# Column sums of a conditioning vector: a rearrangement through DRAM and two four-column products in place of eight one-column products

## The chip, the cores and the metric

The kernel runs on one core of a Trainium2 chip. The metric is the device time of one execution in microseconds (us); the time before is the median of three runs. Five engines of the core work side by side, each through its own list of instructions in order: TensorE (PE, matrix products, with its weight loads listed as PEld), VectorE (DVE), ScalarE (ACT), GpSimd (POOL) and SyncE (SP, which here only issues DMA transfers). An instruction waits at the head of its list until the semaphores it asks for have been raised, and everything behind it on that engine waits with it.

## What is computed

The reference is one decoder block on a sequence of 256 tokens with 2048 channels. A conditioning vector `c` gives six modulation vectors of 2048 numbers each; they scale and shift the two normalisations and gate the two residual branches:

```python
c_act = jax.nn.silu(c)
mod = (c_act @ w_ada[l] + b_ada[l])[:, None, :]
sh1, sc1, g1, sh2, sc2, g2 = jnp.split(mod, 6, axis=-1)
h = rms_norm(x, norm1_g[l]) * (1.0 + sc1) + sh1
x = x + g1 * hybrid_mixer(h, ...)      # sparse attention and a state-space scan, merged, then w_out
h = rms_norm(x, norm2_g[l]) * (1.0 + sc2) + sh2
x = x + g2 * swiglu(h, w_gate[l], w_up[l], w_down[l])
```

All data are float32. The change touches only how `g1`, `sh2`, `sc2` and `g2` are summed. They are wanted late: `g1` first where the output projection `w_out` is added to x, `sc2` and `sh2` at the second normalisation, `g2` in the last projection.

## The kernel before

Nearly all the time goes into products of a weight matrix with the 256 tokens. Weights come in pieces of 128 x 2048 (1 MB, one `entry` each), loaded by SP into one of three `raw` buffers. ACT copies a piece rounded into `wh` (L181), DVE subtracts to get the remainder `wl` (L182); each has three buffers. PE then multiplies `wh` with a 512-column operand (both halves of the split tokens, L207) and `wl` with 256 columns (L208), 16 such pairs for a piece; where the operand is split otherwise, three products of 256 columns take their place (L210 to L212). `run_jobs` processes the entries two jobs ahead of the product. The sums land in four PSUM banks (`acc`); DVE and ACT evacuate them (L251, L252 and others). Smaller products use the four other banks (`ps_side`).

The later modulation is computed beside this, entry by entry. `bg` is a queue of 64 background entries, 8 for each of 8 groups: four vectors `v` in the order 0 (g1), 2 (sc2), 1 (sh2), 3 (g2), in two halves of 1024 channels. An entry is one 1 MB piece of `w_ada`, in the same `raw` buffers as the weights. `ada2_entry.fn` multiplies its two 128 x 1024 halves with columns of `cact` on DVE and adds them up in `acc2`, a tile with a single buffer (pool `bgp`), L430 and L432. After the eighth entry `acc2` holds, in each of 128 partitions, a partial sum for each of 1024 channels. What is left is a sum over partitions, and PE does it (L436): eight products, each with 128 channels of `acc2` as stationary operand and one column of ones as moving operand, into eight columns of a side bank, in which a partition then stands for a channel. A float32 product runs on PE as two passes with a weight load each, so a group has 16. DVE adds the bias into `mods` (L439) and in some groups scales (L442, L444). Where the entries are placed is set by the order of the program, but the order on each engine is made by a scheduler at build time, which pulls instructions ahead of others where it expects waits.

Names used later: a group is written as vector_half, so 1_1 is the second half of vector 1. `pb` is the state-space branch's projection; its accumulator is evacuated by L1052 (multiplied with a gate `sgr` that is loaded from DRAM), added to `pbacc` by L1053, and split into `mg` by ACT L255 and DVE L256. `out` is the `w_out` projection that follows and reads `mg`. `pa` is the attention branch's projection, evacuated by ACT L251 (`ev`) and DVE L252 (`sa`), then gated by L837. `gu` is the gate and up projection of the FFN.

Of the kernel before, what the change touches and what calls it, by code (L numbers as in the profile page):

```python
# [9 lines left out]
F32 = mybir.dt.float32  # L10
F32R = mybir.dt.float32r
AF = mybir.ActivationFunctionType
ALU = mybir.AluOpType
# [3 lines left out]
P = 128  # L17
# [30 lines left out]
def hybrid_block_kernel(  # L48
# [22 lines left out]
    nc = tc.nc  # L71

    act, dve, pool, pe = nc.scalar, nc.vector, nc.gpsimd, nc.tensor

    def open_pool(stack, name, bufs=1, space=None, side=None):
        kw = {} if space is None else {"space": space}
        if side:
            kw["side"] = side
        if name in ("pa1", "pa2", "pb1", "pb2", "pc", "pf", "psa", "pss", "pa"):
            kw["reuse_waits"] = "tile"  # L80
        return stack.enter_context(tc.tile_pool(name=name, bufs=bufs, **kw))

    cst = open_pool(ctx, "cst")
# [21 lines left out]
    dr = open_pool(ctx, "dr", 1, DRAM)  # L105
    bgp = open_pool(ctx, "bgp")
# [3 lines left out]
    def ps_side(name):  # L110
        return banks["side"].tile([P, 512], F32, tag="ps", name=name)
# [152 lines left out]
    ident = cst.tile([P, P], F32, name="ident")  # L264
    make_identity(nc, ident)
    ones = cst.tile([P, P], F32, name="ones")
    pool.memset(ones, 1.0)
    tri = mxp.tile([P, P], F32, name="tri")
    pool.affine_select(tri, ones, [[1, P]], ALU.is_ge, 0.0, base=0, channel_multiplier=-1)
    rb = cst.tile([32, 16], F32, name="rb")  # L270
    eps = cst.tile([P, 1], F32, name="eps")
    pool.memset(eps, EPS)
    cact = cst.tile([P, 16], F32, name="cact")
# [11 lines left out]
    dve.scalar_tensor_tensor(cact, ctmp, 1.0, cact, op0=ALU.add, op1=ALU.mult)  # L285
    dve.tensor_scalar(cc[:, C_CW : C_CB + 48], cc[:, C_CW : C_CB + 48], 0.5, None, op0=ALU.mult)

    d_z = dr.tile([32, P, L], F32, name="d_z")
    d_sa = dr.tile([16, P, L], F32, name="d_sa")
    d_x1 = dr.tile([16, P, L], F32, name="d_x1")  # L290
# [130 lines left out]
    def ada2_entry(v, half, g):  # L421
        def fn(raw):
            if g == 0:
                state["acc2"] = bgp.tile([P, 1024], F32, tag="acc2", name=f"acc2_{v}_{half}")
            a = state["acc2"]
            for j in range(2):
                k = 2 * g + j
                r = raw[:, 1024 * j : 1024 * j + 1024]
                if k == 0:
                    dve.tensor_scalar(a, r, cact[:, 0:1], None, op0=ALU.mult)  # L430
                else:
                    dve.scalar_tensor_tensor(a, r, cact[:, k : k + 1], a, op0=ALU.mult, op1=ALU.add)  # L432
            if g == 7:
                ps = ps_side(f"ada2_{v}_{half}")
                for b in range(8):
                    pe.matmul(ps[:, b : b + 1], a[:, b * P : b * P + P], ones[:, 0:1], start=True, stop=True)  # L436
                o = C_BADA + 16 * (v + 2) + 8 * half
                s = slice(8 * half, 8 * half + 8)
                dve.tensor_tensor(mods[:, v, s], ps[:, 0:8], cc[:, o : o + 8], op=ALU.add)  # L439
                if v == 2:  # L440
                    o = C_N2 + 8 * half
                    dve.scalar_tensor_tensor(a2[:, s], mods[:, 2, s], 1.0, cc[:, o : o + 8], op0=ALU.add, op1=ALU.mult)  # L442
                if v in (0, 3):
                    dve.tensor_scalar(mods[:, v, s], mods[:, v, s], 0.5, None, op0=ALU.mult)  # L444

        entries.append((ada2[16 * v + 8 * half + g], fn))
# [827 lines left out]
    for i, (a, b) in enumerate(OUTC):  # L1274
        eng, f = (pool, r) if a >= OUTP else (dve, rp)
        v = Fd["x2"][:, a:b]
# [112 lines left out]
```

## Time and profile before

| | us |
|---|---|
| median of 3 runs | 2046.61 (2041.5 to 2046.69) |
| the profiled execution | 2048.57 |
| its span, first to last instruction | 2046.9 |
| PE busy | 2011.2 (98%) |
| DVE busy | 1458.3 (71%) |
| ACT busy | 1048.8 (51%) |

The profiled execution took 2048.57 us, of which 1.67 us lie outside the span. A row of a timeline gives the start of a group of instructions of one line, its length, the engine, the line, what is written and read, the count, and in brackets the idle time of the engine ahead of it with what ended it. Lengths of PE rows overlap (an instruction starts before the one ahead of it has drained), so the time that PE needs for some instructions is the distance of the starts, not the sum of the lengths.

### The profile page before, as it was taken

What the parts mean: (1) busy time and instruction counts of PE and PEld (TensorE: products, weight loads), DVE (VectorE), ACT (ScalarE), POOL (GpSimd) and SP (SyncE); (2) the same over time, 40 slices, a digit from 0 to 9 for tenths busy, and PEclk for the clock granted to TensorE, in tenths of its full rate; (3) what the DMA queues carried; (4) which work ended last, traced back from release to release, by engine and by line L of the source; (5) the groups of instructions that cost most, each with busy time, mean ns of one, the idle gap of its engine ahead of it and who ended that gap; (6) DMA issues with size and microseconds to landing.
All of it is one profiled execution on the core that took longest, in us unless ns stands there. A gap on an engine that the chain in (4) does not pass through costs nothing.

```text
span 2046.9 us, 31891 instructions
## 1 busy us (share of the span) xinstructions
PE 2011.2 (98%) x12964; PEld 1794.5 (88%) x12964; DVE 1458.3 (71%) x1832; ACT 1048.8 (51%) x1427; POOL 187.0 (9%) x161
## 2 busy tenths in 40 slices
PE   8999999999999999999999999999999999999997
PEld 6899998899888888889989988888888888888887
DVE  6777787977678888988788765767776555544443
ACT  3665475565346776666664444544444444443442
POOL 0000000230000111100114224000000000000000
PEclk8999999999999999999999999999999999999999
DMA  9888767666887767766577876457775555565552
GB/s 365 331 302 306 269 230 270 218 227 242 300 316 268 255 245 259 255 227 240 210 260 250 283 239 212 166 208 290 259 286 206 185 185 185 200 214 186 187 187 97
DMA packets 102338, 492.29 MB, mean 241 GB/s; under 512 B 10768, under 2 KB 45952, under 8 KB 48688
## 3 DMA queue, kind: packets, MB, share of 16 engines
q1 hardware_dynamic: 100528, 486.19, 66.2%
q0 software_dynamic: 704, 3.15, 0.4%
q8 instruction: 102, 1.67, 0.3%
q10 hardware_dynamic: 960, 0.92, 0.1%
q14 instruction: 44, 0.36, 0.0%
HBM read 475.44 MB, written 17.92 MB: 241 GB/s over the span
## 4 chain that ended last, share of the span: by engine, by line
PE 91%; DVE 4%; DMA 2%; ACT 1%; issue 1%; POOL 0%; SPq 0%; DVEq 0%; POOLq 0%; ACTq 0%
PE acc_gu L207 15%; PE acc_cv L207 9%; PE acc_gu L208 8%; PE acc_dn L207 8%; PE acc_z L207 6%; PE acc_cv L208 4%; PE acc_dn L208 4%; PE acc_pa L207 3%; PE acc_z L208 3%; PE cyc L712 3%; PE cyc L710 3%; PE acc_out L207 3%; PE cyc L711 3%; PE acc_pa L208 2%; PE acc_pb L210 1%; PE acc_pb L212 1%
## 5 line engine op out<-in xcount | busy, mean ns | idle before, releaser
L182 DVE TENSOR_TENSOR wl<-raw,wh 128x2048 fp32r<-128x2048 f32 (+1 forms) x316 | 721.0, 2282 | 364.2 <-ACT wh L181 363.1
L181 ACT ACTIVATE wh<-raw 128x2048 fp32r<-128x2048 f32 (+1 forms) x316 | 599.3, 1898 | 407.0 <-PE acc_dn L207 99.7
L207 PE MATMUL acc_gu<-h,wh 128*128 128x512 f32 x1312 | 463.9, 399 | 0.0
L208 PE MATMUL acc_gu<-h,wl 128*128 128x256 f32 x1312 | 368.5, 281 | 0.0
L207 PEld LDWEIGHTS acc_gu<-h,wh 128*128 128x128 f32 x1312 | 246.5, 188 | 61.5
L207 PE MATMUL acc_cv<-h,wh 128*128 128x512 f32 x768 | 281.4, 407 | 0.0
L208 PEld LDWEIGHTS acc_gu<-h,wl 128*128 128x128 f32 x1312 | 247.8, 189 | 0.0
L207 PE MATMUL acc_dn<-ffact,wh 128*128 128x512 f32 x660 | 233.2, 396 | 0.0
L208 PE MATMUL acc_cv<-h,wl 128*128 128x256 f32 x768 | 217.2, 283 | 0.0
L208 PE MATMUL acc_dn<-ffact,wl 128*128 128x256 f32 x660 | 186.1, 282 | 0.0
L207 PE MATMUL acc_z<-h,wh 128*128 128x512 f32 x512 | 184.1, 401 | 0.0
L207 PEld LDWEIGHTS acc_cv<-h,wh 128*128 128x128 f32 x768 | 145.7, 190 | 38.7 <-issue 4.7
L432 DVE SCALAR_TENSOR_TENSOR acc<-raw,cact,acc 128x1024 f32<-128x1024 f32 x120 | 156.0, 1300 | 2.1 <-DMA raw<-in_ada_dram 1.6
L710 PE MATMUL cyc<-h,wh 128*128 128x256 f32 x512 | 147.8, 289 | 5.1 <-ACT cyc L685 1.8
L207 PEld LDWEIGHTS acc_dn<-ffact,wh 128*128 128x128 f32 x660 | 124.0, 188 | 29.9
L712 PE MATMUL cyc<-h,wl 128*128 128x256 f32 x512 | 144.9, 288 | 3.4 <-DVE wl L182 3.4
L208 PEld LDWEIGHTS acc_cv<-h,wl 128*128 128x128 f32 x768 | 146.6, 191 | 1.0 <-issue 1.0
L210 PE MATMUL acc_pb<-y,wh 128*128 128x256 f32 x512 | 145.9, 285 | 1.0 <-DVE sgr L1052 1.0
L711 PE MATMUL cyc<-h,wh 128*128 128x256 f32 x512 | 146.3, 286 | 0.0
L208 PE MATMUL acc_z<-h,wl 128*128 128x256 f32 x512 | 143.6, 281 | 0.0
L212 PE MATMUL acc_pb<-y,wl 128*128 128x256 f32 x512 | 143.2, 280 | 0.0
L211 PE MATMUL acc_pb<-y,wh 128*128 128x256 f32 x512 | 143.1, 279 | 0.0
(329 smaller groups left out, 3669.7 us busy)
## 6 DMA issues: line engine op xcount, KB each, us to landing
raw<-in_w_gu_dram SPq DMA_DIRECT2D x88, 1024.0 KB, 4.7
raw<-in_ada_dram SPq DMA_DIRECT2D x75, 1024.0 KB, 5.2
raw<-in_w_ssm_dram SPq DMA_DIRECT2D x48, 1024.0 KB, 5.1
raw<-in_w_dn_dram SPq DMA_DIRECT2D x44, 1024.0 KB, 4.7
raw<-in_w_z_dram SPq DMA_DIRECT2D x32, 1024.0 KB, 4.9
raw<-in_w_pb_dram SPq DMA_DIRECT2D x32, 1024.0 KB, 4.9
raw<-in_w_s_dram SPq DMA_DIRECT2D x27, 1024.0 KB, 6.3
raw<-in_w_pa_dram SPq DMA_DIRECT2D x16, 1024.0 KB, 5.3
```

Source lines behind the costliest of these rows:

```text
L181: act.activation(whf[:, o], raw[:, o], AF.Copy)
L182: dve.tensor_tensor(wlf[:, o], raw[:, o], whf[:, o].bitcast(F32), op=ALU.subtract)
L207: pe.matmul(acc, wh, rhs, start=first, stop=last)
L208: pe.matmul(acc[:, :L], wl, rhs[:, :L], start=False, stop=last, skip_group_check=True)
L210: pe.matmul(acc, wh, rhs[:, :L], start=first, stop=False)
L211: pe.matmul(acc, wh, rhs[:, L:], start=False, stop=False)
L212: pe.matmul(acc, wl, rhs[:, :L], start=False, stop=last)
L432: dve.scalar_tensor_tensor(a, r, cact[:, k : k + 1], a, op0=ALU.mult, op1=ALU.add)
L710: pe.matmul(acc, wh[:, t], h[:, k, :L], start=first, stop=False, skip_group_check=True)
L711: pe.matmul(acc, wh[:, t], h[:, k, L:], start=False, stop=False, skip_group_check=True)
L712: pe.matmul(acc, wl[:, t], h[:, k, :L], start=False, stop=(c == n - 1), skip_group_check=True)
```

## The change

At the end of a group, the tile `acc2` (128 x 1024, 512 KB) is written to a DRAM tensor `d_mod`. Four transfers of 128 KB read it back into a tile `fold` of 128 x 8 x 128: the partition 32 g + r of `fold` holds eight pieces of 128 channels, from the four partitions 4 r to 4 r + 3 of `acc2`. `fold` has the tag `acc2` and so takes its one buffer. DVE adds the upper four of the eight pieces to the lower four, then the upper two to the lower two. Two pieces of 128 channels remain, each in four blocks of 32 partitions, and PE sums each block by a product with `pick`, a 128 x 4 matrix with ones where the row belongs to the block. `pick` is made once, by a sum over the identity matrix on DVE near the start. The results stand in the same eight columns of the side bank as before.

```diff
+    pick = cst.tile([P, 4], F32, name="pick")
+    dve.tensor_reduce(pick, ident.rearrange("p (g a) -> p g a", g=4), mybir.AxisListType.X, ALU.add)
...
+    d_mod = dr.tile([P, 1024], F32, name="d_mod")
...
             if g == 7:
+                nc.sync.dma_start(d_mod, a)
+                f = bgp.tile([P, 8, P], F32, tag="acc2", name=f"fold{v}_{half}")
+                for g4 in range(4):
+                    src = bass.AP(d_mod.tensor, d_mod.offset + g4 * P, [[4096, 32], [512, 8], [1, P]])
+                    nc.sync.dma_start(f[32 * g4 : 32 * g4 + 32], src)
+                dve.tensor_tensor(f[:, 0:4], f[:, 0:4], f[:, 4:8], op=ALU.add)
+                dve.tensor_tensor(f[:, 0:2], f[:, 0:2], f[:, 2:4], op=ALU.add)
                 ps = ps_side(f"ada2_{v}_{half}")
-                for b in range(8):
-                    pe.matmul(ps[:, b : b + 1], a[:, b * P : b * P + P], ones[:, 0:1], start=True, stop=True)
+                for b in range(2):
+                    pe.matmul(ps[:, 4 * b : 4 * b + 4], f[:, b], pick, start=True, stop=True)
```

In the changed kernel the transfer to `d_mod` is L439, those from it L443, the two additions L444 and L445, and the product L448. Other lines have moved: L430 and L432 are L433 and L435 there, the bias addition L439 is L451, L444 is L456, L837 is L849, L1052 and L1053 are L1064 and L1065.

The scheduler orders the engines anew around each of the eight places. On DVE at group 1_1, near the end of `pb`, it stood before (the sums of `pb` end with acc_pb3_7_15; wl263 and wl264 are remainders for the second and third piece of `out`):

```order
L1052 SCALAR_TENSOR_TENSOR sgr_11966<-sgr_11966,acc_pb3_5_11_11968 128x256
L1053 TENSOR_TENSOR pbacc_5955<-pbacc_5955,sgr_11966 128x256
L1052 SCALAR_TENSOR_TENSOR sgr_12021<-sgr_12021,acc_pb3_6_12_12023 128x256
L1053 TENSOR_TENSOR pbacc_5955<-pbacc_5955,sgr_12021 128x256
L182 TENSOR_TENSOR wl263_12086<-raw263_12001,wh263_12085 128x2048
```

And with the change:

```order
L182 TENSOR_TENSOR wl263_12101<-raw263_12014,wh263_12100 128x2048
L182 TENSOR_TENSOR wl264_12169<-raw264_12030,wh264_12168 128x2048
L444 TENSOR_TENSOR fold1_1_12019<-fold1_1_12019 128x512
L1064 SCALAR_TENSOR_TENSOR sgr_12036<-sgr_12036,acc_pb3_6_12_12038 128x256
L445 TENSOR_TENSOR fold1_1_12019<-fold1_1_12019 128x256
L1065 TENSOR_TENSOR pbacc_5962<-pbacc_5962,sgr_12036 128x256
L1064 SCALAR_TENSOR_TENSOR sgr_12063<-sgr_12063,acc_pb3_6_13_12065 128x256
L451 TENSOR_TENSOR mods_113<-ada2_1_1_12026,cc_91 128x8
```

The evacuation of acc_pb3_6_12 has moved from ahead of wl263 to behind wl264 and the first addition of the fold.

On PE at the same group, before, the eight products stood in the middle of `pb`:

```order
L211 MATMUL acc_pb3_5_11_11968<-y_11534,wh258_11799 128x256
L212 MATMUL acc_pb3_5_11_11968<-y_11534,wl258_11800 128x256
L436 MATMUL ada2_1_1_12005<-ones_101,acc2_1_1_9984 128x1 x8
L210 MATMUL acc_pb3_6_12_12023<-y_10680,wh259_11867 128x256
L211 MATMUL acc_pb3_6_12_12023<-y_10680,wh259_11867 128x256
```

With the change the two products stand four accumulators later, behind the first product of `out`, whose accumulator acc_out0_0 takes the bank of acc_pb3_6_12:

```order
L211 MATMUL acc_pb3_7_15_12133<-y_11547,wh260_11948 128x256
L212 MATMUL acc_pb3_7_15_12133<-y_11547,wl260_11949 128x256
L207 MATMUL acc_out0_0_12173<-mg_11607,wh262_12032 128x512
L448 MATMUL ada2_1_1_12026<-pick_106,fold1_1_12019 128x4 x2
L208 MATMUL acc_out0_0_12173<-mg_11607,wl262_12033 128x256
L207 MATMUL acc_out0_0_12173<-mg_11607,wh262_12032 128x512
```

So the place of the sum has moved down PE's list, from ahead of acc_pb3_6_12 to behind acc_pb3_7_15.

On DVE at group 0_1, in the attention branch's projection `pa`, it stood before (wl133 is the remainder for acc_pa10):

```order
L182 TENSOR_TENSOR wl131_5501<-raw131_5436,wh131_5500 128x2048
L837 SCALAR_TENSOR_TENSOR sa_5492<-sgar_5457,sa_5492 128x256
L182 TENSOR_TENSOR wl133_5553<-raw133_5498,wh133_5552 128x2048
L252 TENSOR_TENSOR sa_5539<-acc_pa7_7_5506,ev_5540 128x256
L837 SCALAR_TENSOR_TENSOR sa_5539<-sgar_5504,sa_5539 128x256
```

And with the change:

```order
L252 TENSOR_TENSOR sa_5546<-acc_pa7_7_5513,ev_5547 128x256
L444 TENSOR_TENSOR fold0_1_5446<-fold0_1_5446 128x512
L849 SCALAR_TENSOR_TENSOR sa_5499<-sgar_5464,sa_5499 128x256
L445 TENSOR_TENSOR fold0_1_5446<-fold0_1_5446 128x256
L451 TENSOR_TENSOR mods_113<-ada2_0_1_5453,cc_91 128x8
L433 TENSOR_SCALAR acc2_2_0_5554<-raw132_5458,cact_110 128x1024
L456 TENSOR_SCALAR mods_113<-mods_113 128x8
L435 SCALAR_TENSOR_TENSOR acc2_2_0_5554<-raw132_5458,cact_110,acc2_2_0_5554 128x1024
L252 TENSOR_TENSOR sa_5598<-acc_pa8_8_5565,ev_5599 128x256
L849 SCALAR_TENSOR_TENSOR sa_5546<-sgar_5511,sa_5546 128x256
L182 TENSOR_TENSOR wl133_5560<-raw133_5505,wh133_5559 128x2048
```

Here wl133 has moved behind the fold, the first chunk of the next group (L433, L435) and the evacuation of acc_pa8.

## Rows read from the trace of the kernel before

**Rows 1.** The page: busy time of each engine, and the chain that ended last.

```profile
PE 2011.2 (98%) x12964; PEld 1794.5 (88%) x12964; DVE 1458.3 (71%) x1832; ACT 1048.8 (51%) x1427; POOL 187.0 (9%) x161
...
PE 91%; DVE 4%; DMA 2%; ACT 1%; issue 1%; POOL 0%; SPq 0%; DVEq 0%; POOLq 0%; ACTq 0%
```

**Rows 2.** Line L436 by itself: count, min/median/max ns, first and last start.

```profile
L436 PE MATMUL ada<-ones,acc x128: 164/250/271, 426.9 to 1547.8; 128*128 128x1 f32 x128
```

**Rows 3.** Timeline of PE at group 0_0: start, length, engine, line, tiles, count.

```profile
426.87 1.84 PE L436 MATMUL ada<-ones,acc 128*128 128x1 f32 x16
428.57 0.37 PE L210 MATMUL acc_q<-cqs,wh 128*128 128x256 f32 x1
```

**Rows 4.** Stretches: length, busy PE, PEld, DVE, ACT, POOL, granted clock, DMA share, GB/s.

```profile
809.42:812.83 3.41, 3.41 (x12) 2.85 (x12) 3.41 (x6) 2.82 (x6) 0.00 (x0) 0.50 0.55 204
976.67:980.08 3.41, 3.41 (x12) 2.93 (x12) 2.80 (x3) 0.00 (x0) 0.00 (x0) 0.50 0.15 41
1174.64:1178.05 3.41, 3.41 (x17) 3.41 (x17) 3.41 (x7) 0.75 (x2) 0.00 (x0) 0.50 0.98 365
...
396.41:399.82 3.41, 3.30 (x16) 3.00 (x15) 3.41 (x13) 3.41 (x7) 0.00 (x0) 0.50 0.76 271
```

**Rows 5.** Timeline of PE ahead of the stretch at 396.41.

```profile
394.44 0.33 PE L776 MATMUL pT<-ident,part 128*128 128x128 f32 x1 [1.55 <-DVE part L772]
```

**Rows 6.** The DMA list: tiles, queue, count, KB each, median us to landing.

```profile
d_sga<-part SPq DMA_DIRECT2D x4, 512.0 KB, 5.5
d_sgb<-part SPq DMA_DIRECT2D x4, 512.0 KB, 3.2
...
sgar<-d_sga SPq DMA_DIRECT2D x16, 128.0 KB, 5.3
...
sar<-d_sa SPq DMA_DIRECT2D x16, 128.0 KB, 2.8
```

**Rows 7.** Timeline of SP at group 0_1: one of the engine's DMA issues.

```profile
541.05 0.38 SPq L135 DMA_DIRECT2D raw<-in_ada_dram  x1
```

**Rows 8.** Groups of DVE by shape: tiles, shape, count, busy us, mean ns, idle before.

```profile
L252 DVE TENSOR_TENSOR uv<-acc_gu,ev 128x256 f32<-128x256 f32 x41 | 17.1, 417 | 0.0
...
L925 DVE TENSOR_TENSOR xd<-px,dt 128x512 f32<-128x512 f32 x16 | 10.4, 683 | 0.3 <-PE px L903 0.2
```

**Rows 9.** Timeline of PE: group 0_1, and the instruction behind its sum's new place.

```profile
540.87 1.84 PE L436 MATMUL ada<-ones,acc 128*128 128x1 f32 x16
...
559.27 0.40 PE L207 MATMUL acc_pa<-o,wh 128*128 128x512 f32 x1
```

**Rows 10.** Timelines of DVE and PE in the FFN: wl319, and the job that uses it.

```profile
1463.88 2.29 DVE L182 TENSOR_TENSOR wl<-raw,wh 128x2048 fp32r<-128x2048 f32 x1 [1.02 <-ACT wh L181]
...
1472.70 0.40 PE L207 MATMUL acc_gu<-h,wh 128*128 128x512 f32 x1
```

**Rows 11.** Timeline of PE in `pa`: starts of acc_pa9 and acc_pa10.

```profile
559.62 0.39 PE L207 MATMUL acc_pa<-o,wh 128*128 128x512 f32 x1
...
565.27 0.40 PE L207 MATMUL acc_pa<-o,wh 128*128 128x512 f32 x1
```

**Rows 12.** Groups over the kernel: the products of the scan on DVE.

```profile
L943 DVE TENSOR_TENSOR ar<-ar,cbm 128x1024 f32<-128x1024 f32 x16 | 19.5, 1232 | 0.1
```

**Rows 13.** Timeline of PE at group 1_1 and at the start of `out`.

```profile
1172.81 1.92 PE L436 MATMUL ada<-ones,acc 128*128 128x1 f32 x16 [0.58 <-DVE acc L432]
1174.59 0.52 PE L210 MATMUL acc_pb<-y,wh 128*128 128x256 f32 x1
...
1187.51 0.39 PE L207 MATMUL acc_out<-mg,wh 128*128 128x512 f32 x1
```

**Rows 14.** Timelines of DVE and then ACT at the end of `pb`.

```profile
1182.55 0.41 DVE L1052 SCALAR_TENSOR_TENSOR sgr<-sgr,acc_pb 128x256 f32<-128x256 f32 x1
...
1189.59 2.29 DVE L182 TENSOR_TENSOR wl<-raw,wh 128x2048 fp32r<-128x2048 f32 x1 [1.35 <-ACT wh L181]
...
1187.64 1.92 ACT L181 ACTIVATE wh<-raw 128x2048 fp32r<-128x2048 f32 x1 [3.13 <-issue]
```

## The prediction, made before the changed kernel ran

> **What bounds the kernel now.** I read the page first: PE is busy 98% of the span and DVE 71%, and the chain that ended last runs 91% on PE [rows 1]. So what leaves PE's list shortens the kernel, what DVE or the DMA queues do costs nothing until PE waits for it, and every wait of PE is lost. Then I read the line that the change removes: 128 passes over the kernel, 16 in each of eight groups [rows 2]. Their busy time overlaps, so I go by the starts: at group 0_0 the first pass starts at 426.87 and the next work of PE at 428.57, 1.70 us for 16 passes, 0.106 each [rows 3]; the same reading gives 1.78 at 1_1 [rows 13] and 1.70 to 1.81 over all eight, 13.9 together. Last I read the granted clock. Behind three of the eight groups, 2_1, 1_0 and 1_1, PE runs for 3.41 us at 0.50, the lower level of 1.2 GHz, and does half as much in it as at 2.4 [rows 4]. Behind the other five it stays at the upper level.
>
> **What is removed.** A group keeps 4 passes of 16, two products with two passes. Each pass still loads 128 columns of weights, and I take one with four moving columns at what one with a single column costs, 0.106 us. So twelve passes of sixteen go, and with the 13.9 us of the eight groups together this is 0.75 x 13.9 = 10.4 us. The bound above is the mean of the passes with 512 and 256 columns: the 32 of acc_pa9 run from 559.62 to 565.27, 0.177 each [rows 11]. At that price a group would keep 0.71 us instead of 0.43, and 2.2 us of the gain would be lost; four columns are far nearer to one than to 384.
>
> **The clock.** The dips behind groups 2_1 and 1_0 follow 16 passes with one moving column, which stand there behind other short products. Four passes are a quarter of that. I expect both dips to go, which gives back half of 3.41 us twice, 3.4 us; the bounds are 0 and 3.4. The one behind 1_1 I take up below. The Trainium skill speaks against the change here (TensorE: Matmul & The Clock Gate, section "HAM oscillation — how this bites in real kernels"): a PE that has to wait for data is throttled, and the work behind the wait starts at half the clock. The trace agrees: a wait of 1.55 us for DVE at 394.44 [rows 5] stands ahead of the fourth stretch at 0.50, at 396.41 [rows 4]. [...]
>
> **What is added, in time.** A group adds one write of 512 KB, four issues, four reads of 128 KB, and two additions, before PE can start. From the rows [rows 6]: a write of 512 KB lands in 3.2 to 5.5 us, a read of 128 KB in 2.8 to 5.3; an issue on SP takes about 0.4 [rows 7], so five take 2; the additions take as long as a DVE operation of 128x512, 0.68, and of 128x256, 0.42 [rows 8]. The round trip is 3.2 + 2 + 2.8 + 1.1 = 9.1 us at best and 5.5 + 2 + 5.3 + 1.1 = 13.9 at worst. The rearranged reads have pieces of 512 bytes and no row shows that form; the bounds stand. Against this, the order puts L448 far down PE's list. At 0_1 the old products ran at 540.87, and the new ones stand ahead of what ran at 559.27 [rows 9]: 16.7 us of other work lie between. Counted in the same way, without what has moved behind L448, it is 14 to 20 at the others. So the round trip itself is covered everywhere, by 0.1 us at the worst end. The second cover is the queues. SP stops at the first read until `d_mod` has landed, some 5 us, and the weight loads behind it slip; but `wl` is made well ahead: wl319 was ready at 1466.2 for a job that began at 1472.70, 6.5 us later [rows 10]. So this I take at nothing; without that cover it would be up to 5 us a group. DVE gets 8 x 1.1 = 8.8 us more work, and is idle for 29% of the span. `pick` is one DVE operation of 128x128 at the start, below the 0.42 of one of twice its size [rows 8]; DVE waits for transfers there, and I take nothing. `fold` has the only buffer of `acc2`, so the next group's first chunk must wait until L448 is done; it is taken up to 10 us later and keeps a `raw` buffer so long, which the same slack covers.
>
> **What is added, in order.** What is left is the place at which the additions stand in DVE's list. I walked each group with the durations of before and the new order.
> - 0_0: L445 stands behind wl106, whose rounding now waits for the end of acc_z13; PE arrives some 0.4 us early.
> - 0_1: no wait at L448. But wl133, which stood ahead of the evacuation of acc_pa7, now stands behind the fold, L451, L433, L435 and acc_pa8's evacuation. In PE's new time acc_pa8 ends at about 558.4, ACT takes 0.4 for `ev` and 1.9 for wh133, DVE then 0.8 for two evacuations and 2.3 for wl133: ready at about 563.6, while acc_pa10 wants it at 564.2 (1.1 ahead of the 565.27 of before, where acc_pa9 began at 559.62) [rows 11]. It holds with 0.6 us to spare, and the remainders behind it with about 1.
> - 2_0: the scan's transposes have moved behind L448, and its two DVE products of 1.2 us each [rows 12] come so late that PE waits 1.0 us for the second (0 to 2).
> - 2_1 0.3, 1_0 nothing, 3_0 0.5 and 3_1 0.2, each for L445 behind other DVE work.
>
> These are 2.4 us of waits.
>
> **Group 1_1** is the exception. Before, the products cost 1.78 us, after an idle 0.58 [rows 13], and a dip of 1.7. These go from their place, and PE reaches the end of acc_pb3_7_15 about 3.4 us earlier, at 1184.2. There it needs a bank for acc_out0_0, the one of acc_pb3_6_12. In the kernel before this was evacuated at 1182.55, ahead of wl263 and wl264, which was made at 1189.59 [rows 14]. Now the evacuation stands behind wl264 and L444. The rounding wh264, for wl264, needs a buffer that PE frees only with the last product of acc_pb3_7_15 (before it began at 1187.64, when PE went on to `out` at 1187.51) [rows 13, 14]. So from PE's stop on: 1.92 for wh264, 2.29 for wl264, 0.68 for L444, 0.42 for the evacuation: 5.3 us in which PE has nothing to do, then 0.4 for L445. That is 5.7 us. Work on `mg` behind it comes later too, but `out` has 14 of 16 slices by then. Behind an idle time of this length I expect the lower clock for another 3.41 us, 1.7 us, which takes back the 1.7 of the dip that goes.
>
> **The sum**: -10.4 (passes) - 3.4 (two dips) + 2.4 (short waits) + 5.7 (1_1) = -5.7 us. The profiled execution would go from 2048.57 to 2042.9. It lies 2.0 above the median of 2046.61, so for the median I say 2041. This is close to the 0.3% (6.1 us) that a measurement of this kernel can tell from no change.
>
> **The rivals.**
> A. *The stall at 1_1 doesn't come.* If wh264 finds its buffer earlier or the evacuation doesn't hold the bank, 5.7 us and a dip of 1.7 go from the sum: -13.1 us, 2033.5. For it: the rest of the trace shows hardly any wait on PE. Against it: DVE's list is fixed, and wl264 needs wh264.
> B. *The gain turns into waits.* PE arrives earlier at work whose remainders are set by DVE and ACT, and each group loses what it gained; the dips stay, since a wait takes the place of the passes. No change: 2046.6. For it: every wl of `pa` then hangs on the end of the job before. Against it: `wl` is 6 to 8 us ahead in the FFN and the scan.
> C. *Slower: the remainders in `pa` fall behind.* The order at 0_1 leaves 0.6 us. If the DVE work between the end of a job and its remainder, 4.6 us with 0.8 of evacuations, gets also a pair of L435 (2.6), it is 7.2 to 8 us against a job's 5.65 [rows 11], and PE waits about 1.6 at each of six jobs, acc_pa10 to acc_pa15, with a dip at two: 9.6 + 3.4 = 13 us more, +7.3 in sum, 2054. It decides from a delay of 0.6 us on. For it: the slack is small beside the spread of DMA times. Against it: ACT and DVE are both free there most of the time.
> D. *The sums don't shrink as said*, since two passes with four columns cost as the eight did. Nothing in the order supports it; it would end with the stalls alone, +8 us, 2055.
>
> **How the numbers follow.** The forecast has a chance of 0.47, A 0.18, B 0.2, C 0.1, D 0.05. The forecast's own range, from the bounds of the clock (0 to 3.4 back, one more dip at 2_0 or 0_0) and of the short waits (1 to 5), is 2037 to 2047. The range reaches into A and to the near side of C: 2033 to 2051. The forecast lies on the limit of what counts as faster (2040.5), so a little under half of it falls there, 0.22; with A this is 0.40 for faster. Slower is C and D and little else: 0.13. The rest, 0.47, is within 0.3%.
>
> **What would show it.** In the changed kernel, L448 should have 32 passes of about 0.11 us. PE should be idle for 5 to 6 us ahead of the first product of `out`, released by L1064, with a stretch at 0.50 behind it, and the dips behind 2_1 and 1_0 should be gone. In `pa` PE should not wait for wl133 to wl137. I am wrong if PE doesn't stop at `out` (A), or if it waits for L182 in `pa` (C), or if L448 waits for a DMA transfer at any group, since then the round trip isn't covered.

## The result: the changed kernel is slower, and the profile after

The changed kernel takes 2058.64 us in the median of 8 runs (2049.67 to 2063.28), the kernel before beside it 2043.63 (8 runs, 2041.5 to 2046.69). The ratio is 1.0067, with a 95% interval of 1.0051 to 1.0082: slower by 13.7 us (15.0 between the two medians), where 2041 had been forecast and 2033 to 2051 given as the range. The profiled execution took 2060.51 us, its span is 2058.8, 11.9 longer than before.

The page: busy time of each engine and the chain that ended last, which answer to [rows 1].

```profile
PE 1999.8 (97%) x12868; PEld 1782.3 (87%) x12868; DVE 1468.7 (71%) x1849; ACT 1048.9 (51%) x1427; POOL 194.6 (9%) x161
...
PE 72%; issue 12%; DVE 6%; DMA 5%; ACT 3%; POOL 1%; SPq 0%; DVEq 0%; POOLq 0%; ACTq 0%
```

PE has 96 passes and 11.4 us less to do, yet the span is longer: PE waits more. The new sum by line (count, min/median/max ns, first and last start), to set beside [rows 2]:

```profile
L448 PE MATMUL ada<-pick,fold x32: 167/253/355, 442.3 to 1575.7; 128*128 128x4 f32 x32
```

The 32 passes are there, a pass with four columns as long as one with one column (253 against 250 ns). By the starts, as in the forecast, the four passes of a group take 0.36 to 0.47 us at the upper clock; at 0_1, for example, from 559.93 to 560.30:

```profile
559.93 0.51 PE L448 MATMUL ada<-pick,fold 128*128 128x4 f32 x4
560.30 0.48 PE L207 MATMUL acc_pa<-o,wh 128*128 128x512 f32 x1
```

What PE waited for in the changed kernel (what waited, for what; us in all, times, longest):

```profile
PE acc_z L208 <- DVE wl L182: 6.8, 3, 4.6
PE yn L309 <- POOL ysqa L977: 5.9, 3, 2.3
PE acc_out L207 <- DVE sgr L1064: 5.9, 1, 5.9
...
PE ada L448 <- DVE fold L445: 1.0, 2, 0.7
```

None of the first three lines has a counterpart before. Counted over all gaps above 0.25 us behind its first instruction, PE is idle for 46.2 us instead of 23.7. Now the granted clock in the changed kernel (stretch: length, busy PE, PEld, DVE, ACT, POOL, clock, DMA share, GB/s); the last row of the five covers the place of the dip behind 2_1 in [rows 4]:

```profile
439.04:445.87 6.83, 4.38 (x19) 4.29 (x20) 5.50 (x9) 0.42 (x1) 0.00 (x0) 0.50 0.72 252
698.45:701.87 3.42, 3.42 (x13) 2.94 (x12) 0.16 (x2) 3.41 (x4) 0.00 (x0) 0.50 0.90 367
1009.07:1012.48 3.41, 3.41 (x14) 2.93 (x13) 0.46 (x2) 1.04 (x3) 0.00 (x0) 0.50 0.99 397
1196.80:1203.62 6.82, 4.69 (x16) 4.18 (x17) 5.26 (x13) 0.96 (x3) 0.00 (x0) 0.50 0.70 244
808.00:815.00 7.00, 7.00 (x41) 6.08 (x40) 6.96 (x7) 4.56 (x9) 3.48 (x3) 1.00 0.96 341
```

All four dips of [rows 4] are gone (the one at 396.41 lies ahead of the first group, and 1.7 us of the difference with it), and four others have come, each just behind one of the new waits (2.26 and 2.09 us long) or from the middle of one (4.61 and 5.89). Half of what PE does in them is lost: (6.83 - 2.45 idle)/2 + 1.7 + 1.7 + (6.82 - 2.1 idle)/2 = 8.0 us. The ledger: +22.5 (waits) + 8.0 (new dips) - 6.8 (four old dips) - 10.4 (passes) = +13.3, for a span that is 11.9 longer. It holds for these two executions: which dips appear differs from one execution to the next, as the experiments show below.

**Group 0_0.** Timelines of SP, then DVE, then PE in the changed kernel (start, length, engine, line, tiles, count, idle ahead and what ended it):

```profile
423.25 0.42 SPq L439 DMA_DIRECT2D d_mod<-acc  x1
423.73 0.43 SPq L135 DMA_DIRECT2D raw<-in_ada_dram  x1
432.04 1.28 SPq L443 DMA_DIRECT2D fold<-d_mod  x2
...
438.54 0.69 DVE L444 TENSOR_TENSOR fold<-fold 128x512 f32<-128x512 f32 x1 [6.64 <-DMA fold<-d_mod]
439.15 2.29 DVE L182 TENSOR_TENSOR wl<-raw,wh 128x2048 fp32r<-128x2048 f32 x1
...
441.49 0.58 PE L208 MATMUL acc_z<-h,wl 128*128 128x256 f32 x1 [4.61 <-DVE wl L182]
```

The write is issued at 423.25 and its data land at 432.03, since the queue still carries 1 MB loads; SP issues nothing between 424.2 and 432. The last read lands at 438.42, 15.2 us after the write was issued. DVE stands idle at L444 for 6.64 us, with wl106 behind it, whose `wh` had been ready since 435.1. PE has run out of work at 436.9.

**Group 1_1.** Timelines of SP, ACT, DVE and PE in the changed kernel:

```profile
1181.45 0.43 SPq L439 DMA_DIRECT2D d_mod<-acc  x1
...
1188.67 2.50 SPq L443 DMA_DIRECT2D fold<-d_mod  x4
1191.28 1.01 SPq L1052 DMA_DIRECT2D sgr<-d_sgb  x2
...
1193.62 1.91 ACT L181 ACTIVATE wh<-raw 128x2048 fp32r<-128x2048 f32 x1 [1.43 <-DMA raw<-in_w_out_dram]
...
1195.56 2.29 DVE L182 TENSOR_TENSOR wl<-raw,wh 128x2048 fp32r<-128x2048 f32 x1 [1.05 <-ACT wh L181]
1197.77 0.68 DVE L444 TENSOR_TENSOR fold<-fold 128x512 f32<-128x512 f32 x1
1198.37 0.41 DVE L1064 SCALAR_TENSOR_TENSOR sgr<-sgr,acc_pb 128x256 f32<-128x256 f32 x1
...
1198.93 0.76 PE L207 MATMUL acc_out<-mg,wh 128*128 128x512 f32 x1 [5.89 <-DVE sgr L1064]
```

This is the chain forecast from [rows 14]: wh264, wl264, L444, the evacuation, then PE. Only its head differs: PE stopped at 1193.04, and wh264 started 0.6 us later, when its piece of `w_out` had landed, and not when PE freed a buffer. Two gate loads stand behind the reads as well. The first of them, the gate of acc_pb3_6_12, landed at 1196.81, 3.8 us after PE had stopped. In the kernel before it was the second load of this row (timeline of SP), issued at 1177.11, 14.2 us earlier, and it landed 0.6 us ahead of its use; PE itself reached `out` 5.5 us earlier there.

```profile
1176.56 0.94 SPq L1040 DMA_DIRECT2D sgr<-d_sgb  x2
```

**The scan behind 2_0.** Timelines of SP, POOL and PE in the changed kernel: the last `zr` tile comes so late that POOL waits for it, and with it the norm product `yn` on PE.

```profile
661.04 2.51 SPq L443 DMA_DIRECT2D fold<-d_mod  x4
...
685.65 0.42 SPq L967 DMA_DIRECT2D zr<-d_z  x1
...
683.92 0.74 POOL L973 TENSOR_TENSOR xc<-xc,zr 128x256 f32<-128x256 f32 x1 [2.62 <-DVE xc L972]
...
694.26 1.13 POOL L973 TENSOR_TENSOR xc<-xc,zr 128x256 f32<-128x256 f32 x1 [3.92 <-DMA zr<-d_z]
...
697.50 0.60 PE L309 MATMUL yn<-ones,ysqa 128*128 128x1 f32 x4 [2.26 <-POOL ysqa L977]
```

Before, POOL waited for no `zr` there (the same operation ran at 683.66 as soon as DVE had released it) and PE had no wait at `yn`. But this `zr` doesn't stand right behind the reads: they were issued 22 us ahead of it, with eight other issues between. `zr` has two buffers, and its load had to wait until POOL's product at 683.92 had freed one; before, that product ran at 677.23, and both times DVE released it. So the load went 7.6 us later than before (685.65 against 678.05) mostly because DVE's work ahead of it came later, and then it took 8.5 us to land instead of 4.9. That SP's stop made it late is not shown.

### The profile page after: what moved, and what is told of

Same layout as the page of the kernel before. It is cut to its first block, busy times and chain, and to the rows that moved or that the text cites. A ratio compares the mean times of both kernels' runs of the same rounds, so it can differ in the third digit from the quotient of the medians.

```text
span 2058.8 us, 31769 instructions
## 1 busy us (share of the span) xinstructions
PE 1999.8 (97%) x12868; PEld 1782.3 (87%) x12868; DVE 1468.7 (71%) x1849; ACT 1048.9 (51%) x1427; POOL 194.6 (9%) x161
## 3 DMA queue, kind: packets, MB, share of 16 engines
q8 instruction: 101, 1.65, 0.3%
## 4 chain that ended last, share of the span: by engine, by line
PE 72%; issue 12%; DVE 6%; DMA 5%; ACT 3%; POOL 1%; SPq 0%; DVEq 0%; POOLq 0%; ACTq 0%
PE acc_gu L207 14%; PE acc_dn L207 7%; PE acc_gu L208 7%; PE acc_cv L207 5%; PE acc_dn L208 4%; PE acc_out L207 3%; PE acc_cv L208 3%; PE cyc L724 2%; PE cyc L722 2%; PE cyc L723 2%; PE acc_pa L207 2%; DVE wl L182 2%; PE acc_z L207 2%; ACT wh L181 1%; PE acc_out L208 1%
## 5 line engine op out<-in xcount | busy, mean ns | idle before, releaser
L435 DVE SCALAR_TENSOR_TENSOR acc<-raw,cact,acc 128x1024 f32<-128x1024 f32 x120 | 156.1, 1301 | 12.5 <-DMA raw<-in_ada_dram 12.0
```

## The experiments

Two theories went into the first runs. The order (theory 1): the additions stand ahead of remainders and evacuations on DVE, and PE waits for these. The stop (theory 2): the reads hold SP until `d_mod` has landed, and what SP loads just in time comes late. Diffs are against the changed kernel, those of the two versions with a transpose against the kernel before; ratios are to the kernel before, timed on the same chip. Differences in microseconds are between medians unless a ratio is named. The scheduler orders every one of these programs anew, so that none of them changes one thing alone.

**The transfers alone.** The old eight products, then the write and the four reads into `fold`, which nothing uses.

```diff
+                ps = ps_side(f"ada2_{v}_{half}")
+                for b in range(8):
+                    pe.matmul(ps[:, b : b + 1], a[:, b * P : b * P + P], ones[:, 0:1], start=True, stop=True)
                 nc.sync.dma_start(d_mod, a)
...
-                dve.tensor_tensor(f[:, 0:4], f[:, 0:4], f[:, 4:8], op=ALU.add)
-                dve.tensor_tensor(f[:, 0:2], f[:, 0:2], f[:, 2:4], op=ALU.add)
-                ps = ps_side(f"ada2_{v}_{half}")
-                for b in range(2):
-                    pe.matmul(ps[:, 4 * b : 4 * b + 4], f[:, b], pick, start=True, stop=True)
```

> The eight one-column products stay as they were, and after them each group still writes its partial sums to DRAM and reads them back into the shared buffer; nothing reads them there. This is the DMA part of the change alone: SP's stop, the traffic and the blocked buffer, with no engine's additions or products waiting for it. Theory 1 (place: what costs is that work stands behind the fold in the lists of DVE and PE and waits for its transfers): within 4 us of the kernel before, 2040 to 2048, and no waits of PE at acc_z, yn or out. Theory 2 (queue: SP's stop and the traffic make weight pieces and gates late, whatever the order): most of the 15 us between the kernels is here, plus the 10 us that the shorter products gave: 2055 to 2070.

2053.92 us (2049.13 to 2060.54), ratio 1.0055 (1.0033 to 1.0077). Its waits on PE:

```profile
PE acc_out L207 <- DVE sgr L1062: 4.7, 1, 4.7
PE yn L309 <- POOL ysqa L975: 4.1, 2, 2.5
...
PE acc_z L208 <- DVE wl L182: 1.6, 2, 1.3
```

Transfers that nobody reads cost 10.8 us and bring the waits at `out` and `yn` without an addition; the order of DVE has the evacuation behind wl264 here too. Only the long wait at 0_0 is missing. The time lies 1 us under the range of theory 2 and 6 over that of theory 1. So the additions can't be the whole cause: much of the loss comes without them, and so does the order at `out`.

**The arithmetic alone.** The rearrangement is left out; the additions and the four-column products work on `acc2` as it lies.

```diff
-                nc.sync.dma_start(d_mod, a)
-                f = bgp.tile([P, 8, P], F32, tag="acc2", name=f"fold{v}_{half}")
-                for g4 in range(4):
-                    src = bass.AP(d_mod.tensor, d_mod.offset + g4 * P, [[4096, 32], [512, 8], [1, P]])
-                    nc.sync.dma_start(f[32 * g4 : 32 * g4 + 32], src)
+                f = a.rearrange("p (q j) -> p q j", q=8)
```

> The additions and the two four-column products run on the tile of partial sums as it lies, without the rearrangement through DRAM (the rearrangement is left out, so the four vectors are wrong sums). This is the arithmetic of the change without its latency. Theory 1: the passes give 10 us and the dips behind 2_1, 1_0 and 1_1 another 3 to 5, with no new waits: 2028 to 2034. A third theory (the additions on DVE or the four-column products themselves cost): 2040 or more. Theory 2 expects the same as theory 1 here.

2032.75 us (2026.99 to 2038.25), ratio 0.9953 (0.9933 to 0.9973). The waits at acc_z, `yn` and `out` are gone; the new one on PE is

```profile
PE ada L444 <- DVE acc L441: 4.3, 4, 2.0
```

What the change saves is there, 10.4 us below the kernel before; all of the loss comes with the way through DRAM. From this kernel to the changed one it is some 25 us. The transfers alone make up 10.8; the other 12 to 15 (by ratios or by medians) come only where the additions and products wait for the reads. No run has that part by itself. In the traces the wait at 0_0 with its dip (6.8 us) belongs to it, and the rest is not assigned.

**Traffic or stop.** First the write alone, behind the old products:

```diff
+                ps = ps_side(f"ada2_{v}_{half}")
+                for b in range(8):
+                    pe.matmul(ps[:, b : b + 1], a[:, b * P : b * P + P], ones[:, 0:1], start=True, stop=True)
                 nc.sync.dma_start(d_mod, a)
...
-                    nc.sync.dma_start(f[32 * g4 : 32 * g4 + 32], src)
...
-                for b in range(2):
-                    pe.matmul(ps[:, 4 * b : 4 * b + 4], f[:, b], pick, start=True, stop=True)
```

> The eight one-column products as before, and after them only the write of 512 KB of each group to DRAM; nothing is read back. The first runs showed that the DMA part alone costs 11 us, and that loads of the gates stand on SP behind the four reads, which wait for the write to land. Theory 2a (stop: SP's list stands still at the reads, and what is behind them comes late): no read, no stop, so within 3 us of the kernel before, 2040 to 2046. Theory 2b (traffic: the added bytes slow the loads): the write is half of the bytes, so 4 to 6 us, 2047 to 2050.

2042.8 us, ratio 1.0006 (0.9992 to 1.0021): no cost that shows. In its trace the sixteen passes at 2_1 and 1_0 take 1.79 and 1.81 us as before, and yet PE stays at the upper clock behind them (stretches from the end of the passes on, read as in [rows 4]):

```profile
805.94:810.00 4.06, 4.06 (x25) 3.58 (x25) 3.89 (x8) 3.23 (x8) 0.00 (x0) 1.00 0.55 227
971.80:976.00 4.20, 4.20 (x32) 3.41 (x32) 3.19 (x4) 0.14 (x1) 0.43 (x1) 1.00 0.66 211
```

Then the first experiment again, with the reads issued by POOL (the line that differs from it):

```diff
-                    nc.sync.dma_start(f[32 * g4 : 32 * g4 + 32], src)
+                    nc.gpsimd.dma_start(f[32 * g4 : 32 * g4 + 32], src)
```

> The eight one-column products as before, the write and the four reads of each group as in the change, with no one using them, but the reads are issued by POOL in place of SP. Theory 2a: SP doesn't stop any more; POOL does, and its work on y in the scan is what can come late: 2041 to 2048. Theory 2b: as with the reads on SP, 2052 or more.

2045.45 us, ratio 1.0016 (0.9999 to 1.0033). The same bytes move, and the loss falls from 0.55% to 0.16%. So most of the loss hangs on the reads standing in SP's list, not on the traffic. It fits SP standing still at a transfer that isn't ready; the order that the scheduler builds around the reads changes with them, and this run doesn't separate the two.

**Place by place.** The old sum at some groups, the changed one at the others. At 1_1 only the old sum:

```diff
+                if (v, half) == (1, 1):
+                    ps = ps_side(f"ada2_{v}_{half}")
+                    for b in range(8):
+                        pe.matmul(ps[:, b : b + 1], a[:, b * P : b * P + P], ones[:, 0:1], start=True, stop=True)
+                else:
+                    nc.sync.dma_start(d_mod, a)
...
```

> The change in seven groups; group 1_1 alone keeps its eight one-column products. Theory 1: the 5.9 us wait of PE ahead of out goes with some 2.4 us of half clock behind it and 1.0 us at the two products, and 1.3 us of passes and perhaps a dip of 1.7 come back: 4 to 8 us less than the changed kernel, 2051 to 2055. Theory 2: the wait at out came from late gates and pieces that seven folds still delay; under 3 us less, 2056 to 2059.

2054.14 us, ratio 1.0051 (1.0032 to 1.007); the wait of 5.9 us at `out` is gone (0.4 is left), acc_z (6.8 us) and `yn` (5.6) stay. The changed sum in the FFN alone:

```diff
+                if v != 3:
...
```

> The change in the two groups of the FFN alone (3_0 and 3_1); the other six keep the eight one-column products. Theory 1: nothing stands behind the fold there, so the passes' 2.5 us are gained less 0.3 to 1 of waits: 1.5 to 2.5 us below the kernel before, 2041 to 2042. Theory 2: SP stops there too, 2043.6 or more.

2039.92 us, ratio 0.998 (0.9971 to 0.9989). In the scan and the FFN:

```diff
+                if v == 0 or (v, half) == (1, 1):
...
```

> The change in the three groups of the scan (2_0, 2_1, 1_0) and the two of the FFN; 0_0, 0_1 and 1_1 keep the eight one-column products. With the kernels that changed the FFN alone (2039.9) and all but 1_1 (2054.1), this splits the loss by stage. Theory 2a together with theory 1: half of the loss is in attention (0_0 with 4.6 us of wait and its half clock, and the pieces in pa), so 8 us go: 2044 to 2048. If the scan has nearly all of it (its yn waits): 2050 or more. If attention has nearly all of it: 2036 to 2041.

2043.95 us, ratio 1.0005 (0.9988 to 1.0022). In the attention branch alone:

```diff
+                if v != 0:
...
```

> The change in 0_0 and 0_1 alone; the six later groups keep the eight one-column products. If the losses of the stages add up (all but 1_1 is 10.2 us above scan and FFN), these two groups lose by themselves 8 to 12 us: 2051 to 2056, with the waits at acc_z14, acc_pa and the first acc_z of the scan and the half clock after the first. If they lose only together with the later groups: 2043 to 2048.

2050.59 us, ratio 1.0042 (1.0027 to 1.0058), with the wait at acc_z (5.8 us, longest 4.0) and the dip of 6.83 us behind it. FFN and attention have their own runs, -0.20% and +0.42%; the others follow by differences, scan +0.25% (1.0005 less 0.998) and 1_1 +0.16% (1.0067 less 1.0051). The sum, +0.63%, meets the +0.67% of the whole.

**0_0: order or round trip.** The additions of 0_0 and 0_1 go to POOL, so that wl106 can't stand behind them.

```diff
-                dve.tensor_tensor(f[:, 0:4], f[:, 0:4], f[:, 4:8], op=ALU.add)
-                dve.tensor_tensor(f[:, 0:2], f[:, 0:2], f[:, 2:4], op=ALU.add)
+                add = pool if v == 0 else dve
+                add.tensor_tensor(f[:, 0:4], f[:, 0:4], f[:, 4:8], op=ALU.add)
+                add.tensor_tensor(f[:, 0:2], f[:, 0:2], f[:, 2:4], op=ALU.add)
```

> The whole change, with the two additions of groups 0_0 and 0_1 on POOL in place of DVE, so that wl106 no longer stands behind an addition that waits for the reads; in PE's list the two products of 0_0 now stand ahead of acc_z14. Theory D (DVE's list: PE waits at 0_0 only because wl106 stands behind the addition): PE's wait of 4 to 5 us there is gone, with its 6.83 us at half clock: 5 to 7 us less than the changed kernel, 2050 to 2054. Theory R (round trip: the reads land after PE has run out of other work, whatever the list): the wait stays, at the two products, 4 to 6 us: 2056 to 2061.

2055.69 us, ratio 1.0072 (1.0049 to 1.0095). PE now waits for the sum itself:

```profile
PE ada L449 <- POOL fold L446: 4.4, 1, 4.4
...
PE acc_z L208 <- DVE wl L182: 2.0, 2, 1.5
```

The time lies between the two ranges, and the run is no clean test of the two theories. POOL's first addition starts at 439.62, when the reads are in, and PE stands at the two products from 437.3 on. But the remainder wl106 came early, as theory D wanted (DVE in this run):

```profile
436.93 2.29 DVE L182 TENSOR_TENSOR wl<-raw,wh 128x2048 fp32r<-128x2048 f32 x1 [3.69 <-ACT wh L181]
```

It was ready at 439.2, and acc_z14, which uses it, stood behind the two products in PE's list, with acc_q ahead of it; neither needs the sum. So this order only moves the wait from wl106 to the sum. Whether PE would run dry with wl106 ahead of the additions and the products behind acc_z14 was not run.

**Two attempts to mend it.** The reads, additions and products are written one background entry later, behind other loads on SP:

```diff
             if g == 0:
+                if "fin" in state:
+                    state.pop("fin")()
...
                 nc.sync.dma_start(d_mod, a)
+
+                def fin():
+                    f = bgp.tile([P, 8, P], F32, tag="acc2", name=f"fold{v}_{half}")
...
+                state["fin"] = fin
```

> The whole change, with the reads, the additions and the products written into the program one background entry later, just before the next group takes the buffer (1_1 in the second job of out, 3_1 where it was). On SP one to nine other issues now stand between the write and the first read. Theory 2a: the write has landed or nearly when SP comes to the reads, so the stop and the loads that were late behind it go, some 10 us, and the passes' gain stays: 2040 to 2049. Theory 1 alone: as in the changed kernel, the work behind the fold waits for the same round trip, only later: 2052 or more.

2051.88 us, ratio 1.0044 (1.0028 to 1.0059): some 5 us better than the change (1.0067), on the edge between the two theories, with waits of 6.7 us at the sum, 6.5 at `yn` and 2.4 at `out`. Ahead of the first read SP now stands still for under 0.1 us in six groups, but still for 8.3 us at 0_0 and 4.0 at 3_1. In the scan the stop there is gone and the waits at `yn` are not, so they don't hang on it alone. And the whole change with the reads issued by POOL (the one line of the experiment above):

> The whole change, with the four reads of each group issued by POOL in place of SP. Theory 2a: the 11 us of the DMA part go or nearly, while what stands behind the fold on DVE and PE stays (0_0 above all): 2044 to 2050, and PE's wait ahead of out is gone or under 2 us. Theory 2b: 2055 or more. Theory 1 alone (place) expects no difference to the changed kernel, 2056 to 2060.

2078.67 us, ratio 1.0182 (1.0162 to 1.0203). This missed. The scheduler now places the products earlier, and PE waits for the round trip at all eight groups:

```profile
PE ada L448 <- DVE fold L445: 25.0, 8, 7.4
```

**The same sum without DRAM.** DVE transposes `acc2` in blocks of 32 x 32 in place, sums each block's rows, and PE adds the four blocks with a 128 x 32 selection.

```diff
+    sel = cst.tile([P, 32], F32, name="sel")
+    dve.tensor_reduce(sel, ident.rearrange("p (g c) -> p c g", g=4), mybir.AxisListType.X, ALU.add)
...
+                dve.transpose(a, a)
+                r32 = bgp.tile([P, 32], F32, tag="r32", name=f"r32_{v}_{half}")
+                dve.tensor_reduce(r32, a.rearrange("p (b e) -> p b e", e=32), mybir.AxisListType.X, ALU.add)
...
+                for j in range(4):
+                    pe.matmul(ps[32 * j : 32 * j + 32, 0:8], sel, r32[:, j:32:4], start=True, stop=True)
```

> A rearrangement without DRAM: DVE transposes the 128 x 1024 partial sums in squares of 32 x 32 in place and sums each 32 elements, which leaves 128 x 32; four products with a selection matrix of 32 columns as stationary operand sum the four blocks of partitions. PE keeps 8 passes of 16, each with a weight load of a quarter of the columns, and no transfer is waited for; DVE gets about 2.5 us a group. Theories 2a and 2b alike: no stop, no traffic, so the gain of the passes shows, 8 to 11 us, and up to 5 us of dips: 2027 to 2035, and faster than both kernels. If what costs is DVE's extra work or the later place of the product, 2040 or more.

2036.15 us in the median of 12 runs, ratio 0.9966 (0.9951 to 0.9981): faster than both kernels, and 1 us over the range that was expected. Groups of DVE in it (count, busy us, mean ns, idle before), then its waits on PE:

```profile
L438 DVE STREAM_TRANSPOSE acc<-acc 128x1024 f32<-128x1024 f32 x8 | 9.9, 1239 | 0.1
L440 DVE TENSOR_REDUCE r<-acc 128x32 f32<-128x1024 f32 x8 | 9.7, 1211 | 0.1
```

```profile
PE ada L443 <- DVE r L440: 5.1, 3, 2.5
...
PE yn L308 <- POOL ysqa L972: 2.9, 2, 1.5
```

20 us of work on DVE cost PE 5.1 us of waits at the sum. Ahead of the first wait at `yn` stands POOL's wait for `zr` again, with no transfer through `d_mod` in the program (POOL in this run, behind 2_0):

```profile
687.93 3.96 POOL L968 TENSOR_TENSOR xc<-xc,zr 128x256 f32<-128x256 f32 x1 [2.76 <-DMA zr<-d_z]
```

To win the 5.1 us back, the four products of this version were written two jobs later:

```diff
+                def late():
+                    j0 = state.get("job", 0)
+                    for _ in range(8):
+                        if state.get("job", 0) >= j0 + 2:
+                            break
+                        yield
...
+                gens.append(late())
```

> The rearrangement on DVE without DRAM as in the kernel that ran at 2036.2, with the products and the bias addition written into the program two jobs later, so that PE doesn't stand waiting for DVE's sums (5.1 us in all there). Theory 2a and 1 alike: those 5 us and two dips of 1.7 behind them go: 2027 to 2034. If PE's waits only move elsewhere: 2036 or more.

2037.6 us, ratio 0.9973 (0.9959 to 0.9987). The wait at the sum is gone, but waits at `yn` (3.6) and in `pb` (1.7 and 1.3) stand in its place: no gain. Last, the changed kernel was profiled once more.

> The changed kernel once more, for a second trace. If the waits belong to the program's order and not to one execution, PE waits again for wl106 at acc_z (4 to 5 us), for sgr ahead of out (5 to 6 us) and for ysqa at three yn (5 to 6 us together): 2050 to 2063.

2061.32 us, with waits of 5.9 us at acc_z, 5.8 at `yn` and 5.7 at `out`: they belong to the program, not to one execution.

Not tried: a buffer of its own for `fold`, which takes 4 KB in each partition (8 x 128 numbers of 4 bytes).

## Why the prediction was wrong, point by point

By stage, the forecast's own terms (1.3 us of passes a group, the dips, the waits) against the runs, a ratio of 0.1% being 2.04 us. The intervals of the runs leave 2 to 5 us of doubt in each measured value, so that the one of 1_1 is not clear of zero:

| stage | forecast, us | measured, us |
|---|---|---|
| attention: 0_0, 0_1 | -2.6 + 0.4 = -2.2 | +8.6 |
| scan: 2_0, 2_1, 1_0 | -3.9 - 3.4 + 1.3 = -6.0 | +5.1 |
| 1_1 | -1.3 + 5.7 = +4.4 | +3.3 |
| FFN: 3_0, 3_1 | -2.6 + 0.7 = -1.9 | -4.1 |

- **The passes: right.** 32 are left, 0.36 to 0.47 us for the four of a group at the upper clock where 0.43 was forecast. That the arithmetic alone also came out 10.4 us faster is luck in part: 4.3 us of waits at the sum are in it, and dips that come and go.
- **The clock: partly luck on what goes, too low on what comes.** The dips behind 2_1 and 1_0 went. But they were read from one execution and taken as a cost of the sixteen passes. Six traces have the sixteen passes at these two groups (the kernel before, the transfers alone, their version with POOL, the write alone, FFN alone, attention alone): behind 2_1 four of them have a dip, behind 1_0 two. So a gain of 3.4 us from the change is not shown. Of the new dips only one was counted, at 1_1, where four came, worth 8.0 us. The sentence on the Trainium skill (TensorE: Matmul & The Clock Gate, section "HAM oscillation — how this bites in real kernels"), that work behind a wait for data starts throttled, is borne out by the trace in all four. Not every wait is followed by one: the 1.80 us at 612.98 and the 1.60 at 874.06 are not, while in the second trace of the same kernel the second of them, 1.65 us long there, is.
- **"SP stops at the first read ... So this I take at nothing": the first step that failed.** The evidence was one weight piece with 6.5 us to spare [rows 10]. The stop came: ahead of the first read SP issued nothing for 7.9 us at 0_0, 6.3 at 2_1, 4.2 at 1_0 and 3_0, 2.9 at 1_1 and 0.7 to 2.5 at the others, 3.8 on average. But SP also loads the gate tiles `sgr` and `zr`, and those had nothing to spare: before, the gate of acc_pb3_6_12 landed 0.6 us ahead of its use, and the last `zr` behind 2_0 0.7. For `sgr` at 1_1 the trace shows the load right behind the reads; for `zr` it does not. With no addition in the program the transfers cost 10.8 us; with the reads off SP's list, 3.6. So the term that was put at nothing is worth some 7 us, whether by the stop itself or by the order built around it. The end "up to 5 us a group" stood in the text and was dropped on the ground of the one load that was looked at.
- **"The round trip itself is covered everywhere, by 0.1 us at the worst end": the second.** From the write's issue to the last landing with the additions left out, it took 10.2 to 16.2 us in the eight groups, against 8.0 to 12.8 in the sum without its 1.1 of additions. The write was priced by writes that land in 3.2 to 5.5 us [rows 6]; here its median is 6.7, behind 1 MB loads in the same queue, and an issue of a read takes 0.6, not 0.4. At 0_0 the 15.2 us and the 1.1 of the additions stand against some 14 us that PE had to do ahead of L448 (from the write's issue at 423.25 to 436.9, and one pair of acc_z14): about 2 us short, an estimate from these rows. The two medians:

```profile
d_mod<-acc SPq DMA_DIRECT2D x8, 512.0 KB, 6.7
fold<-d_mod SPq DMA_DIRECT2D x32, 128.0 KB, 4.6
```

- **0_0, 0.4 us forecast, 4.6 and a dip of 2.2 measured.** The walk saw L445 behind wl106 and did not ask what stood ahead of wl106: L444, which waits for the reads. The run with the additions on POOL moved the wait to the sum, since the products stood ahead of acc_z14 there; an order with neither in the way was not run.
- **1_1: right, with 5.89 us of idle time against 5.3, and half clock behind it.** The steps of the chain came as worked out, though PE came to this place at 1193.0 and not at 1184.2, since it had waited further up; the 0.6 us more are the wait of wh264 for its piece of `w_out`. The cause given for its order, the additions, is only part of it: the transfers alone, without L444, put the evacuation behind wl264 as well and cost 4.7 us there.
- **The scan: missed.** It was given 1.3 us of waits at the products; the waits came later, at `yn` (5.9 us), with two dips. The transfers alone bring 4.1 of it, the arithmetic alone none. But the version with the transpose, which has no transfers, has 2.9 there, behind the same wait of POOL for `zr`; and with the stop gone in the scan 6.5 were left. What makes `zr` late in each version stays open.
- **The rivals.** None is what happened. B came nearest in kind, a gain that turns into waits, but was priced to end at no change, since only remainders were asked for slack. C named the right sign in the wrong place: in `pa` PE waits for `wl` 0.5 us in all. The wait of 1.80 us for `wl` at 612.98, behind `pa`, was in no rival, and its cause was not followed. "Wrong if L448 waits for a DMA transfer" was the right warning with the wrong instruction to look at: L448 hardly waits (1.0 us), since the wait shows at wl106, ahead of it.

## What to carry to other kernels

A transfer that depends on fresh results, put on the queue that issues all loads, stops every load behind it until those results have landed (7.9 us at 0_0); check the slack of the small tiles that are loaded just in time, not only that of the big pieces. Price a transfer by others that stand behind the same traffic, and walk back from each instruction that PE needs to everything ahead of it on its engine until nothing waits. Where a sum over partitions is to leave PE, a block transpose and a reduction on DVE keep it on the core: here 2036.15 us against 2041.88 for the kernel before beside it, where the way through DRAM took 2058.64 against 2043.63. Price a dip of the clock only when more than one profile shows it.

## What the runs showed of the hardware

The write of 512 KB alone showed no cost (ratio 1.0006, 0.9992 to 1.0021), though it shares the queue with the loads; the reads cost 10.8 us with the write when SP issued them and 3.6 when POOL did. The lower clock behind the same sixteen passes came in some executions and not in others (behind 2_1 in four traces of six). The 32 x 32 transpose of 128 x 1024 numbers in place takes 1.24 us on DVE, as long as a product of that shape there (1.23 [rows 12]), and the sum over blocks 1.21.
